# Two column blocks of the shared values by seven half-size products instead of eight, with the modulation sums 1024 columns wide

## The chip, the core and the metric

The kernel runs on one core of a Trainium2 chip. The metric is the time of one execution on the device in microseconds. Before the change the median of 3 runs is 1925.47 us (1925.35 to 1926.13).

## What is computed

A decoder trunk of two layers over 512 tokens and 2048 features, all float32. Layer A is a differential attention, layer B a forgetting attention that reads keys, values and gates projected once from the output of layer A. Cut to what matters here:

```python
def shared_kv(x, c_act, w_mod_kv, b_mod_kv, w_kv, b_f):
    mod = c_act @ w_mod_kv + b_mod_kv
    shift, scale = jnp.split(mod, 2, axis=-1)
    hk = x * (1.0 + scale[:, None]) + shift[:, None]
    kvf = hk @ w_kv
    k, v, zf = jnp.split(kvf, [B_WIDTH, 2 * B_WIDTH], axis=-1)
...
for l in range(DEPTH):
    mod = c_act @ w_mod[l] + b_mod[l]
    shift, scale, gate = jnp.split(mod, 3, axis=-1)
    h = x * (1.0 + scale[:, None]) + shift[:, None]
    y = diff_attention(h, ...) if l < N_A else forgetting_attention(h, ..., k_sh, v_sh, F_sh)
    x = layer_norm(DN_ALPHA * x + gate[:, None] * y, ln_g[l], ln_b[l])
```

`kvf` is a product of 512 x 2048 by 2048 x 4112: 2048 columns of keys, 2048 of values, 16 of gate logits. Each `mod` is a matrix-vector product over 2048 rows, which VectorE sums up beside the large products.

## The kernel before

Every large product is made of 128 x 128 x 512 matmuls in fp32r. For accuracy each operand is split into a rounded part and a rest (`hi`, `lo`), and `products` (L206) issues three matmuls: hi by hi, hi by lo, lo by hi. So a block of 512 columns costs 16 depth tiles x 4 token blocks x 3 = 192 matmuls.

`WeightStream` (L67) brings the weights, in the order of the list `ws.order`. One step is a tile `wst` of two depth tiles by 512 columns (512 KB, four buffers), loaded through the SP queue; ScalarE casts it to `whi` (L113), VectorE subtracts to get `wlo` (L114), three buffers each. `ws.get` keeps the splitting two steps ahead of the product.

`group` (L345) runs one column block: for each of 8 weight steps, 4 bursts of 6 matmuls. After each burst `tick` runs one waiting piece (attention, evacuations) and, where `bg` says so, some steps of `background`. That is `mod_stream` (L396): it loads 512 columns of a modulation weight and multiplies them into the accumulator `macc` on VectorE (L433), one depth tile per step. The first such stream, opened at L818, runs beside layer A's projections (the groups `qk[h]` and `vg[h]`) and makes the gate of layer A and the shift and scale of the keys and values. The second, opened in `open_n` (L1262), runs from layer A's output projection on and makes layer B's shift, scale and gate; part of its loads go through tiles `msk` of the pool `K`.

The normalised output of layer A is one tile `n`, 4 token blocks by 2048 columns. `build_half` (L1318) turns it on TensorE, scales it on ScalarE and splits it to `Hh`, `Hl`, and writes the turned values back to `n`; six of the 32 pieces go through DRAM in place of TensorE. `build_h` (L1373) reads the turned `n` once more for layer B.

The value columns are five blocks `vj`: 0, 512 and 1024 (512 wide), 1536 and 1800 (264 wide, the last with the gate logits). Below they are called V0 to V4, and the four key blocks `kj` K0 to K3. V0 is built by hand together with `build_half`; V1 to V4 (L1474) and K0 to K3 (L1477) are groups, in this order. The tile framework decides where each instruction stands on its engine, apart from those that are kept in program order; within an engine execution is in order, and a waiting instruction holds all behind it.

## Time and profile before

| what | us |
|---|---|
| median of 3 runs | 1925.47 |
| span of the profiled execution, first to last instruction | 1923.5 |
| difference, around the span | 1.97 |
| PE busy | 1910.4 |
| DVE (VectorE) busy | 1370.3 |
| ACT (ScalarE) busy | 732.9 |
| V1 to V4, from the end of V0 to the end of V4 | about 131 |

PE is TensorE's matmuls, PEld its weight loads, SP the queue that issues most DMAs. A view of windows gives busy time in a stretch, in us from the span's start; the number in brackets behind it counts instructions, and the last three numbers are the granted clock as a share of full speed, the share of time that the DMA engines were busy, and GB/s. A view of groups gives the busy sum, the mean duration in ns, and the idle time ahead of the group with what ended it. A timeline row gives start and duration. Matmuls overlap, so the duration of one is not the time it adds.

### The profile page before, as it was taken

To read this page: it belongs to the slowest core of one execution; us is meant where nothing else is said; L and a number is where in the kernel's file an instruction comes from. 1 tells how busy PE (TensorE), PEld (TensorE's weight loads), DVE (VectorE), ACT (ScalarE), POOL (GpSimd) and SP (SyncE) were. 2 spreads that over 40 slices of the span, in tenths; PEclk is the share of its full clock that TensorE was granted. 3 is DMA by queue.
4 is the path that set the end of the run, shared out by engine and by line. 5 is a ranking of instruction groups with operands and counts; after the bars stand their busy time and mean duration, and the time that the engine had idled before them with its cause. 6 is when DMAs were issued, how large, how long until landed. Compare 5 with 4: busy or idle time off the path is not lost.

```text
span 1923.5 us, 25879 instructions
## 1 busy us (share of the span) xinstructions
PE 1910.4 (99%) x8921; PEld 1593.5 (83%) x8921; DVE 1370.3 (71%) x2617; ACT 732.9 (38%) x1266; POOL 2.3 (0%) x11
## 2 busy tenths in 40 slices
PE   8999999999999999999999999999999999999998
PEld 7888888888888888888888898888888888888887
DVE  8993578777676868667675477777566666686768
ACT  3656344333232344521272232224344444453122
POOL 0000000000000000000000000000000000000000
PEclk9999999999999999999999999999999999999999
DMA  9993566676767675476557586775355555555622
GB/s 346 385 333 95 160 186 196 213 234 196 228 203 224 207 223 180 122 241 222 179 165 256 181 294 211 258 258 160 114 149 156 161 149 160 154 154 170 224 93 110
DMA packets 352275, 382.22 MB, mean 199 GB/s; under 512 B 77912, under 2 KB 256244, under 8 KB 351376
## 3 DMA queue, kind: packets, MB, share of 16 engines
q1 hardware_dynamic: 349040, 376.23, 62.2%
q10 hardware_dynamic: 3104, 4.35, 0.6%
q8 instruction: 70, 1.15, 0.3%
q14 instruction: 61, 0.50, 0.1%
HBM read 348.68 MB, written 31.80 MB: 198 GB/s over the span
## 4 chain that ended last, share of the span: by engine, by line
PE 97%; DVE 1%; SPq 1%; DMA 0%; issue 0%; ACT 0%; ACTq 0%
PE acc L208 27%; PE acc L210 27%; PE acc L209 27%; PE acc L720 4%; PE sc L720 2%; PE sc L210 1%; PE sc L209 1%; PE sc L208 1%; PE o L208 1%; PE o L210 1%; PE o L209 1%; PE o L720 1%; SPq L568 0%; PE tr L686 0%; PE tr L660 0%; DMA sms<-in_w_mod_dram 0%
## 5 line engine op out<-in xcount | busy, mean ns | idle before, releaser
L113 ACT CAST whi<-wst 128x1024 fp32r<-128x1024 f32 (+2 forms) x298 | 303.4, 1018 | 617.6 <-PE acc L210 310.1
L114 DVE TENSOR_TENSOR wlo<-wst,whi 128x1024 fp32r<-128x1024 f32 (+2 forms) x298 | 351.4, 1180 | 248.8 <-ACT whi L113 228.9
L208 PE MATMUL acc<-hh,whi 128*128 128x512 f32 x1184 | 462.9, 391 | 0.0
L209 PE MATMUL acc<-hl,whi 128*128 128x512 f32 x1184 | 461.6, 390 | 0.0
L210 PE MATMUL acc<-hh,wlo 128*128 128x512 f32 x1184 | 460.0, 390 | 0.0
L208 PE MATMUL acc<-whi,hh 128*128 128x512 f32 (+1 forms) x1104 | 418.5, 379 | 0.0
L209 PE MATMUL acc<-wlo,hh 128*128 128x512 f32 (+1 forms) x1104 | 416.7, 377 | 0.0
L210 PE MATMUL acc<-whi,hl 128*128 128x512 f32 (+1 forms) x1104 | 416.2, 377 | 0.0
L433 DVE SCALAR_TENSOR_TENSOR macc<-ms,cact,macc 128x512 f32<-128x512 f32 x307 | 229.0, 746 | 63.0 <-DMA ms<-in_w_mod_dram 44.5
L210 PEld LDWEIGHTS acc<-hh,wlo 128*128 128x128 f32 x1184 | 222.3, 188 | 47.4
L208 PEld LDWEIGHTS acc<-hh,whi 128*128 128x128 f32 x1184 | 222.3, 188 | 44.0 <-DVE sgb L1509 0.8
L209 PEld LDWEIGHTS acc<-hl,whi 128*128 128x128 f32 x1184 | 222.5, 188 | 42.3
L210 PEld LDWEIGHTS acc<-whi,hl 128*128 128x128 f32 x1104 | 207.3, 188 | 38.9
L208 PEld LDWEIGHTS acc<-whi,hh 128*128 128x128 f32 x1104 | 207.3, 188 | 37.2 <-DVE ztmp L1241 0.6
L209 PEld LDWEIGHTS acc<-wlo,hh 128*128 128x128 f32 x1104 | 207.4, 188 | 36.0
L618 DVE SCALAR_TENSOR_TENSOR sacc<-sms,cact,sacc 128x512 f32<-128x512 f32 (+1 forms) x128 | 89.9, 703 | 4.6 <-DMA sms<-in_w_mod_dram 0.7
L904 ACT ACTIVATE e<-e,mn 128x128 f32<-128x128 f32 (+3 forms) x64 | 36.0, 563 | 109.5 <-DVE mn L900 102.9
L1559 ACT ACTIVATE eb<-eb,mnb 128x128 f32<-128x128 f32 (+1 forms) x64 | 35.9, 561 | 72.7 <-DVE mnb L1556 72.4
L720 PE MATMUL acc<-wlo,hh 128*128 128x512 f32 x128 | 49.8, 398 | 0.0
L720 PE MATMUL acc<-whi,hl 128*128 128x512 f32 x128 | 49.3, 393 | 0.0
L720 PE MATMUL acc<-whi,hh 128*128 128x512 f32 x128 | 49.2, 393 | 0.0
L132 DVE TENSOR_TENSOR wlo<-wst,whi 128x768 fp32r<-128x768 f32 (+1 forms) x32 | 34.8, 1088 | 17.8 <-ACT whi L125 16.5
(336 smaller groups left out, 2096.6 us busy)
## 6 DMA issues: line engine op xcount, KB each, us to landing
wst<-in_a_w_in_dram SPq DMA_DIRECT2D x240, 256.0 KB
ms<-in_w_mod_dram SPq DMA_DIRECT2D x136, 256.0 KB
ms<-in_kv_w_mod_dram SPq DMA_DIRECT2D x64, 512.0 KB
wst<-in_b_w_in_dram SPq DMA_DIRECT2D x128, 256.0 KB
sms<-in_w_mod_dram SPq DMA_DIRECT2D x56, 512.0 KB
wst<-in_kv_w_dram SPq DMA_DIRECT2D x56, 512.0 KB
ms<-in_w_mod_dram SPq DMA_DIRECT2D x32, 512.0 KB
wst<-in_a_w_out_dram SPq DMA_DIRECT2D x32, 512.0 KB
```

The costliest lines, as they stand in the source:

```text
L113: self.nc.scalar.copy(hi[:, :, :w], st[:, :, :w])
L114: self.nc.vector.tensor_tensor(lo[:, :, :w], st[:, :, :w], hi[:, :, :w].bitcast(F32), op=ALU.subtract)
L132: self.nc.vector.tensor_tensor(lo[:, :, :w], st[:, :, :w], hi[:, :, :w].bitcast(F32), op=ALU.subtract)
L208: PE.matmul(dst, lhs[0], rhs[0], start=start, stop=False, skip_group_check=True)
L209: PE.matmul(dst, lhs[0], rhs[1], start=False, stop=False, skip_group_check=True)
L210: PE.matmul(dst, lhs[1], rhs[0], start=False, stop=stop, skip_group_check=True)
L433: ins = V.scalar_tensor_tensor(acc, w, cact[:, kt : kt + 1], acc, op0=ALU.mult, op1=ALU.add)
L618: V.scalar_tensor_tensor(acc, w, sc, acc, op0=ALU.mult, op1=ALU.add)
L720: PE.matmul(bank[n, bk], l, r, start=start, stop=stop, skip_group_check=True)
L904: S.activation(e[:, :w], e[:, :w], AF.Exp, bias=mn, scale=-1.0, accum_out=rs)
L1559: S.activation(e[:, :w], e[:, :w], AF.Exp, bias=mn, scale=-1.0, accum_out=rs)
```

## The change

V1 and V2 are now computed together as a product of 2 x 2 blocks, with seven half-size products instead of eight (Winograd's variant of Strassen's scheme). The activations are cut by tokens (blocks 0, 1 and 2, 3) and by even and odd depth tiles, the weights by even and odd depth tiles and by column block.

- `combine(s)` makes, for depth tiles 2s and 2s+1, four combinations of the activations (`sums`), split to `su` and `sl`. `su` takes the memory of `n`, which is therefore saved to `s_dram` and read back by `back_n`.
- `PairFirst` and `PairSecond` feed the weight stream: 4 steps of plain even tiles, 8 steps with one subtraction, 16 steps in pairs with three subtractions per pair, all on VectorE in the raw tile. During them every third raw tile is a `wsp` in the memory of the `ms` tiles, so that up to six are in use.
- `seven_products` has three phases: p1 (48 matmuls), p7 and p3 (96), and p2, p7, p1, p3 together (192).
- The order is now V0, V3, V4, the pair, K0 to K3. In the pair no `tick` runs, so no step of the modulation either.
- The modulation streams work on tiles of 1024 columns, with one `macc`, and layer B's gate has moved to the first stream. `bg` is set anew in all groups. The tiles `msk` are gone.
- `n` is four tiles of 512 columns, so `norm_a` issues two activations instead of one, two scalings instead of one, and four stores instead of one per token block.

```diff
+class PairFirst:
+    def load(self, nc, dst, kt):
+        n = kt // 2
+        if n < 4:
+            rows = self.src[4 * n * P : (4 * n + 4) * P, self.c0 : self.c0 + 512]
+            nc.sync.dma_start(dst, rows.rearrange("(k u p) n -> p k u n", p=P, u=2)[:, :, 0, :])
+        else:
+            rows = self.src[2 * (n - 4) * P : (2 * (n - 4) + 2) * P, self.c1 : self.c1 + 512]
+            nc.sync.dma_start(dst, rows.rearrange("(k p) n -> p k n", p=P))
+    def sums(self, nc, n, st, after):
+        if n >= 4:
+            nc.vector.tensor_tensor(st[:, 0, :], st[:, 1, :], st[:, 0, :], op=ALU.subtract)
...
+class PairSecond:
+    def load(self, nc, dst, kt):
+        n = kt // 2
+        c0 = self.cols[n % 2]
+        rows = self.src[2 * (n // 2) * P : (2 * (n // 2) + 2) * P, c0 : c0 + 512]
+        nc.sync.dma_start(dst, rows.rearrange("(k p) n -> p k n", p=P))
+    def sums(self, nc, n, st, after):
+        if n % 2 == 0:
+            other, minus = after(), partial(nc.vector.tensor_tensor, op=ALU.subtract)
+            minus(other[:, 0, :], other[:, 0, :], st[:, 0, :])
+            minus(other[:, 1, :], other[:, 1, :], other[:, 0, :])
+            minus(st[:, 0, :], st[:, 1, :], other[:, 1, :])
...
-            st = self.pool.tile([P, 2, 512], F32, name="wst", tag="wst", bufs=self.STAGES)
+            if self.paired(len(self.stage)) and len(self.stage) % 3 == 2:
+                st = self.spare()
+            else:
+                st = self.pool.tile([P, 2, 512], F32, name="wst", tag="wst", bufs=self.STAGES)
             job.load(self.nc, st, 2 * s)
             self.stage.append(st)
+    def paired(self, n):
+        return n < len(self.order) and isinstance(self.order[n][0], (PairFirst, PairSecond))
...
+        if isinstance(job, (PairFirst, PairSecond)):
+            self.load(self.done + 2)
+            job.sums(self.nc, s, st, lambda: self.stage[self.done + 1])
...
+            while self.paired(len(self.stage)) and self.paired(self.done) and len(self.stage) < self.done + self.STAGES + 1:
+                self.load(len(self.stage) + 1)
...
+    s_dram = dram.tile([4, P, TB, 512], F32, name="s_dram")
...
+    pair = PairFirst(kv_w, 2048 + 512, 2048 + 1024), PairSecond(kv_w, 2048 + 512, 2048 + 1024)
+    for j in [o[1] for o in oA] + [vj[0], vj[3], vj[4]]:
+        ws.add_job(j)
+    for j, steps in zip(pair, (12, 16)):
+        ws.add_job(j, steps)
+    for j in kj + bj + [o[1] for o in oB]:
         ws.add_job(j)
...
+        for k, (i, kt) in enumerate(todo):
+            load_upto(k if calm else k + ahead)
...
+                ins = V.tensor_scalar(acc, w, one, None, op0=ALU.mult)
+            else:
+                ins = V.scalar_tensor_tensor(acc, w, one, acc, op0=ALU.mult, op1=ALU.add)
+            tc.keep_in_program_order(ins)
+            if kt == 4:
+                while turned_sums:
+                    next(turned_sums.pop(0), None)
+            yield
+            if kt == KT - 1:
+                for half, steps in enumerate(segs[i][2]):
+                    turned_sums.append(steps(acc[:, 512 * half : 512 * half + 512]))
+                    next(turned_sums[-1])
+                    yield
...
+            ap, (
+                (gate_dram[0], w_mod[0], 2 * D, b_mod[0], (0.0,)), (gate_dram[1], w_mod[1], 2 * D, b_mod[1], (0.0,)),
+                (mod_dram[0], kv_w_mod, 0, kv_b_mod, (0.0, 1.0)),
+            ),
+        ),
+        lambda: ap.tile([P, 1024], F32, name="ms", tag="ms", bufs=2),
+        lambda: ap.tile([P, 1024], F32, name="macc", tag="macc", bufs=1),
+        1,
...
-    group(qk[2], False, lambda b, acc: keep(("qk", b), acc), bg=lambda k: k % 3 == 2)
+    group(qk[2], False, lambda b, acc: keep(("qk", b), acc), bg=lambda k: k % 4 == 3)
...
-    group(vg[2], True, keep_vg, bg=lambda k: k % 2)
+    group(vg[2], True, keep_vg, bg=lambda k: k % 3 == 1)
...
-        group(qk[h], False, evac, bg=lambda k: k % 2)
+        group(qk[h], False, evac, bg=lambda k: k % 3 == 1)
...
-        group(vg[h], True, evac_rest, bg=lambda k: 1 if k % 8 in (1, 3, 4, 5, 7) else 0, after_sub=early if h == A_HEADS - 1 else None)
+        group(vg[h], True, evac_rest, bg=lambda k: k % 2, after_sub=early if h == A_HEADS - 1 else None)
...
-            bg = (lambda n: 1 if n % 3 else 0) if layer == 0 and k in (1, 2) else 0
+            bg = (lambda n: n % 3 == 1) if layer == 0 and k in (1, 2) else 0
...
-            deep=range(50, 106),
-            new_deep=lambda: ktile("msk"),
+            vectors(pool, ((mod_dram[1], w_mod[1], 0, b_mod[1], (0.0, 1.0)),)),
+            lambda: pool.tile([P, 1024], F32, name="ms", tag="ms", bufs=3),
+            lambda: pool.tile([P, 1024], F32, name="macc", tag="macc", bufs=1),
+            2,
...
+    def combine(s):
+        cs = 256 * s, 256 * s + 256
+        whole = []
+        for q in range(2):
+            kt = 2 * s + q
+            f = npool.tile([P, T], F32, name="htmp", tag="htmp", bufs=2)
...
+                src = ncols(slice(0, TB), kt * P, (kt + 1) * P)
+                S.activation(f.rearrange("p (b t) -> p b t", t=P), src, AF.Identity, scale=sc, bias=sh)
+            whole.append((f[:, 0:256], f[:, 256:512]))
+        if s % 2:
+            nc.sync.dma_start(s_dram[s // 2], nt[s // 2])
+        sums = npool.tile([P, 4, 256], F32, name="sums", tag="tn", bufs=2)
+        (a11, a21), (a12, a22) = whole
+        s3, s4, s1, s2 = (sums[:, k, :] for k in range(4))
+        V.tensor_tensor(s1, a21, a22, op=ALU.add)
+        V.tensor_tensor(s2, s1, a11, op=ALU.subtract)
+        V.tensor_tensor(s3, a11, a21, op=ALU.subtract)
+        V.tensor_tensor(s4, a12, s2, op=ALU.subtract)
+        waiting.append((s, sums))
+        if s % 2:
+            t = npool.tile([P, 2, 4, 256], F32R, name="su", tag="n", bufs=4)
+            for k, (w, sums) in enumerate(waiting):
+                upper[w] = t[:, k]
+                S.copy(upper[w], sums)
+                lower[w] = [kpool.tile([P, 2, 256], F32R, name="sl", tag="K") for _ in range(2)]
+                for m, lo in enumerate(lower[w]):
+                    two = slice(2 * m, 2 * m + 2)
+                    V.tensor_tensor(lo, sums[:, two], upper[w][:, two].bitcast(F32), op=ALU.subtract)
+            waiting.clear()
...
+    def seven_products():
+        def add(dst, lhs, tiles, k, start=False, stop=False):
+            for b in both:
+                products(dst[b], lhs(b), (tiles[0][k], tiles[1][k]), start, stop)
...
+        p1 = [acc_bank() for _ in both]
+        for a in range(4):
+            tiles = ws.get(one, a)
+            if a < 2:
+                combine(6 + a)
+            for k in range(2):
+                s = 2 * a + k
+                add(p1, lambda b: plain(2 * s, b), tiles, k, s == 0, s == 7)
...
+        for b in both:
+            S.copy(first[b], p1[b])
+        p7 = [acc_bank() for _ in both]
+        p3 = [sc_bank() for _ in both]
+        for s in range(8):
+            tiles = ws.get(one, 4 + s)
+            add(p7, lambda b: combined(s, 0, b), tiles, 0, s == 0, s == 7)
+            add(p3, lambda b: combined(s, 1, b), tiles, 1, s == 0, s == 7)
+        diff = [npool.tile([P, T], F32, name="htmp", tag="htmp", bufs=2) for _ in both]
+        for b in both:
+            S.copy(diff[b], p3[b])
+            V.tensor_tensor(diff[b], p7[b], diff[b], op=ALU.subtract)
...
+        for s in range(8):
+            last = s == 7
+            ta = ws.get(two, 2 * s, 1)
+            add(p2, lambda b: plain(2 * s + 1, b), ta, 1, s == 0, last)
+            if s not in (0, 7):
+                add(p7, lambda b: plain(2 * s + 1, 2 + b), ta, 0)
+            tb = ws.get(two, 2 * s + 1, 1 if s in (0, 7) else 2)
+            add(p1, lambda b: combined(s, 3, b), tb, 1, stop=last)
+            if s in (0, 7):
+                add(p7, lambda b: plain(2 * s + 1, 2 + b), ta, 0, stop=last)
+            add(p3, lambda b: combined(s, 2, b), tb, 0, stop=last)
+            if last:
+                for b in both:
+                    V.tensor_tensor(first[b], p2[b], first[b], op=ALU.add)
...
+                us = [ktile("us") for _ in both]
+                for b in both:
+                    S.copy(us[b], p1[b])
+                for b in both:
+                    t = ktile("vt")
+                    V.tensor_tensor(t, p7[b], us[b], op=ALU.add)
+                    store(t, 2 + b, c0)
+                for b in both:
+                    t = ktile("vt")
+                    V.tensor_tensor(t, p3[b], us[b], op=ALU.add)
+                    store(t, b, c1)
+                    V.tensor_tensor(diff[b], diff[b], t, op=ALU.add)
+                    store(diff[b], 2 + b, c1)
...
+    def back_n():
+        new_n()
+        for f in range(4):
+            nc.sync.dma_start(nt[f], s_dram[f])
...
-    for g in range(1, 5):
-        group(vj[g], True, evac_v(g), bg=lambda k: k % 2)
+    group(vj[3], True, evac_v(3), bg=lambda k: k % 8 == 7, after_sub=lambda s: combine(s // 2) if s in (0, 2, 4) else None)
+    calm.append(1)
+    ws.spare = lambda: npool.tile([P, 2, 512], F32, name="wsp", tag="ms", bufs=3)
+    group(vj[4], True, evac_v(4), bg=lambda k: k in (3, 11), after_sub=lambda s: combine(3 + s // 2) if s in (0, 2, 4) else None)
+    seven_products()
+    calm.clear()
+    back_n()
...
         group(
-            kj[g], False, evac_k(g), bg=lambda k: 1 if k % 4 else 0,
+            kj[g], False, evac_k(g), bg=lambda k: k % 2 or k % 8 == 0,
```

How the instructions move. First TensorE, whose order rests on the products alone. Before, in V1, three matmuls per block and depth tile, all into the four banks `acc` (columns: line, operation, output, moving and stationary operand, size):

```order
L208 MATMUL acc<-whi,hh 128x512
L209 MATMUL acc<-wlo,hh 128x512
L210 MATMUL acc<-whi,hl 128x512
L208 MATMUL acc<-whi,hh 128x512
L209 MATMUL acc<-wlo,hh 128x512
```

And now, at the start of the pair's third phase (`p` are the banks of p2, `acc` of p1 and p7, `sc` of p3; `su`, `sl` are combined activations):

```order
L266 MATMUL p_10082<-whi,hh 128x512
L267 MATMUL p_10082<-wlo,hh 128x512
L268 MATMUL p_10082<-whi,hl 128x512
L266 MATMUL acc<-whi,su 128x512
L267 MATMUL acc<-wlo,su 128x512
L268 MATMUL acc<-whi,sl 128x512
L266 MATMUL acc<-whi,su 128x512
L267 MATMUL acc<-wlo,su 128x512
L268 MATMUL acc<-whi,sl 128x512
L266 MATMUL acc<-whi,hh 128x512
```

The form of the matmul is the same; a weight tile now serves 12 of them, where it served 24. In the whole program TensorE has 8817 matmuls and transposes, where it had 8865: 48 fewer, all of 512 columns.

Next VectorE. Before, between two weight splits of V2 it ran modulation steps (`macc`), and at the end of a sum its turning (`mturn`) and reduction (`mred`):

```order
L433 SCALAR_TENSOR_TENSOR macc<-msk,cact,macc 128x512 x2
L464 STREAM_TRANSPOSE mturn<-macc 128x512
L465 TENSOR_REDUCE mred<-mturn 128x16
L114 TENSOR_TENSOR wlo<-wst,whi 128x1024
L431 TENSOR_SCALAR macc<-msk,cact 128x512
L433 SCALAR_TENSOR_TENSOR macc<-msk,cact,macc 128x512
```

Now, in the third phase of the pair, the subtractions on raw tiles (L108 to L110) stand there:

```order
L169 TENSOR_TENSOR wlo<-wsp,whi 128x1024
L108 TENSOR_TENSOR wst<-wst,wsp 128x512
L109 TENSOR_TENSOR wst<-wst 128x512
L108 TENSOR_TENSOR wsp<-wsp,wst 128x512
L169 TENSOR_TENSOR wlo<-wst,whi 128x1024
L110 TENSOR_TENSOR wsp<-wsp,wst 128x512
L109 TENSOR_TENSOR wsp<-wsp 128x512
L169 TENSOR_TENSOR wlo<-wst,whi 128x1024
L110 TENSOR_TENSOR wst<-wst,wsp 128x512
L169 TENSOR_TENSOR wlo<-wsp,whi 128x1024
```

Per two splits there are three subtractions and no modulation step.

Last ScalarE, near the end of V0, where `build_half` feeds the product. Before, the build's activations and a weight cast:

```order
L1347 ACTIVATE htmp_9193<-sc,mod_b_7741,mod_a_7740 128x256
L1348 ACTIVATE hh<-sc,mod_b_7741,mod_a_7740 128x256
L1332 ACTIVATE hh<-n,mod_b_7741,mod_a_7740 128x256 x2
L113 CAST whi<-wst 128x1024
L1347 ACTIVATE htmp_9253<-sc,mod_b_7741,mod_a_7740 128x256
```

Now, at the same place (`sums` is the output of `combine`, L1483 its own activations):

```order
L1405 ACTIVATE htmp_9166<-sc,mod_b_7757,mod_a_7756 128x256
L1406 ACTIVATE hh<-sc,mod_b_7757,mod_a_7756 128x256
L1483 ACTIVATE htmp<-n,mod_b_7757,mod_a_7756 128x512 x2
L1499 CAST su<-sums 128x1024
L1390 ACTIVATE hh<-n,mod_b_7757,mod_a_7756 128x256
L168 CAST whi<-wst 128x1024
L1390 ACTIVATE hh<-n,mod_b_7757,mod_a_7756 128x256
L1405 ACTIVATE htmp_9226<-sc,mod_b_7757,mod_a_7756 128x256
```

The first activations of `combine` and the first cast to `su`, which waits until the store of the first quarter of `n` to `s_dram` has landed, stand ahead of the last pieces of the build.

172 lines of the change are left out of this document (88 added, 84 removed).

## The prediction

> **What bounds the kernel now.** The page comes first: its span, its busy times, and the chain that ended last.
>
> ```profile
> span 1923.5 us, 25879 instructions
> PE 1910.4 (99%) x8921; PEld 1593.5 (83%) x8921; DVE 1370.3 (71%) x2617; ACT 732.9 (38%) x1266; POOL 2.3 (0%) x11
> PE 97%; DVE 1%; SPq 1%; DMA 0%; issue 0%; ACT 0%; ACTq 0%
> ```
>
> TensorE is the bound from end to end: 97% of the chain. But a busy share of pipelined matmuls proves little, so the view of waits comes second, for TensorE: what did it wait for in the middle of the program?
>
> ```profile
> PE tr L241 <- DMA crow<-in_c_dram: 3.1, 1, 3.1
> PE sc L1339 <- ACT n L1314: 0.2, 1, 0.2
> ```
>
> These are the first and the seventh of its eight waits. Five lie before 195 us, in the preamble, two of 0.3 and 0.2 us behind 1330, where layer B runs. Between them, over the stages that the change touches, only the second of these rows is left: 0.2 us, once. So removing work from any other engine wins nothing, removing matmuls wins their pitch, and every new wait of TensorE is lost time.
>
> Third, the pitch. The timeline of TensorE in V1 gives start and duration; the two rows are 36 matmuls apart:
>
> ```profile
> 1059.82 0.39 PE L208 MATMUL acc<-whi,hh 128*128 128x512 f32 x1
> ...
> 1067.98 0.39 PE L208 MATMUL acc<-whi,hh 128*128 128x512 f32 x1
> ```
>
> (1067.98 − 1059.82) / 36 = 0.2267 us from start to start; the 0.39 us of a record overlaps its neighbours. As a cross-check, the last evacuations of V1 and of V2:
>
> ```profile
> 1063.42 0.59 ACT L1400 COPY vt<-acc 128x512 f32<-128x512 f32 x1 [0.77 <-PE acc L210]
> ...
> 1106.94 0.59 ACT L1400 COPY vt<-acc 128x512 f32<-128x512 f32 x1 [0.77 <-PE acc L210]
> ```
>
> They lie 43.52 us apart for 192 matmuls: 0.2267 again. A column block is pure pitch.
>
> Fourth, the windows: is there room beside TensorE? Columns: window, length, busy time of PE, PEld, DVE, ACT, POOL, clock, DMA share, GB/s.
>
> ```profile
> 455.00:502.00 47.00, 47.00 (x219) 39.27 (x218) 32.12 (x57) 13.46 (x22) 0.00 (x0) 1.00 0.74 230
> 980.00:1020.00 40.00, 39.78 (x191) 32.60 (x190) 24.73 (x50) 26.75 (x50) 0.00 (x0) 1.00 0.49 145
> 1064.00:1108.00 44.00, 44.00 (x201) 36.63 (x200) 21.22 (x26) 10.32 (x14) 0.00 (x0) 1.00 0.58 196
> 1108.00:1156.00 48.00, 48.00 (x390) 47.45 (x390) 38.05 (x53) 14.29 (x25) 0.00 (x0) 1.00 0.87 291
> 1288.00:1332.00 44.00, 44.00 (x195) 36.17 (x195) 38.52 (x69) 20.63 (x30) 0.00 (x0) 1.00 0.57 182
> ```
>
> They are one `vg` group of layer A, V0 with the build, V2, V3 with V4, and the last key block. The granted clock is 1.00 in each. Two rows matter as precedents: V3 and V4 use up a weight step in 2.9 us (16 in 46) and load 291 GB/s without a stall; the last key block has VectorE 88% busy without a stall.
>
> **The change part by part.** *Removed.* V1 and V2 took 384 matmuls, 384 × 0.2267 = 87.0 us. The seven products take 336 of the same form, 76.2 us. Gain **48 × 0.2267 = 10.88 us**. Nothing else on TensorE changes in number.
>
> The row that bears on a rule of the Trainium skill is the timeline above, 226.7 ns with a weight load before each matmul. "TensorE: Matmul & The Clock Gate", section "Back-to-back issue gap", puts a sustained stream of such pairs at about 131 ns for 512 columns; by that the estimate would be 48 × 0.131 = 6.3 us. The trace shows 226.7 over 36 and over 192 matmuls, so it decides; the sum is made with 10.88.
>
> *Added on VectorE and ScalarE in the pair.* The rows, from the groups by form (busy, mean ns):
>
> ```profile
> L114 DVE TENSOR_TENSOR wlo<-wst,whi 128x1024 fp32r<-128x1024 f32 x274 | 334.6, 1221 | 215.6 <-ACT whi L113 199.8 <-PE o L209 6.6 <-DMA e<-turned 4.0
> L113 ACT CAST whi<-wst 128x1024 fp32r<-128x1024 f32 x274 | 288.2, 1052 | 576.0 <-PE acc L210 277.3 <-PE acc L209 211.8 <-issue 50.5
> L114 DVE TENSOR_TENSOR wlo<-wst,whi 128x528 fp32r<-128x528 f32 x16 | 11.3, 707 | 16.1 <-ACT whi L113 11.9 <-DMA msk<-in_w_mod_dram 4.1
> L1241 DVE TENSOR_TENSOR ztmp<-acc,gate 128x512 f32<-128x512 f32 x24 | 15.7, 681 | 1.0 <-PE acc L210 0.9
> L1349 DVE TENSOR_TENSOR hl<-htmp,hh 128x256 fp32r<-128x256 f32 x24 | 10.0, 417 | 7.2 <-ACT hh L1348 7.2
> ```
>
> The pair has 28 weight steps where V1 and V2 had 16. VectorE does 31 splits there, with the first three of K0: 31 × 1.221 = 37.9 us. To these come 8 + 24 subtractions on raw tiles and about 12 operations of 512 columns from `combine` and the evacuations: 44 × 0.681 = 30.0 us. Together 67.9 of 76.2 us, 89%; the last key block ran at 88%. In exchange no modulation step stands in the pair. ScalarE casts 31 × 1.052 = 32.6 us plus some 8 of copies: not a bound. The cover for all of this is TensorE: 12 matmuls per step, 2.72 us. Without it each step costs what VectorE needs above 2.72 us; that is the first rival.
>
> *Added beside V3 and V4.* Six calls of `combine`: 24 additions of 256 columns at 0.417 and 12 subtractions at about 0.68 make 18.2 us of VectorE, with 16 splits of 528 columns (11.3) and 6 modulation steps (7.7, price below) 37 us, with the build's last operations some 42 of 46 us. The row of before has 38.05 there with no stall. So nothing, as long as the splits stay two steps ahead.
>
> *Switches of the banks.* Four places are new: first to second phase, second to third, third to K0, and V4 to the pair; a fifth is V0's end, where ScalarE's queue now holds a cast to `su` that waits for a store, and behind it the last build pieces, on which TensorE waits. Nearest row: the V0 window, PE 39.78 of 40.00, so 0.22 us lost at a similar hand-over. Bounds per place: zero (V2's window, 44.00 of 44.00) and 0.77 + 0.59 us, the wait and the copy of an evacuation row. I take 0.22 × 5 = **1.1 us**; range 0 to 6.8.
>
> *Modulation.* A 1024-wide step has its price from the nearest row of that shape:
>
> ```profile
> L433 DVE SCALAR_TENSOR_TENSOR macc<-ms,cact,macc 128x512 f32<-128x512 f32 x307 | 229.0, 746 | 63.0 <-DMA ms<-in_w_mod_dram 44.5 <-DMA ms<-in_kv_w_mod_dram 15.4
> L1751 DVE SCALAR_TENSOR_TENSOR z<-z,lrstd,ln_b 128x1024 f32<-128x1024 f32 x6 | 7.4, 1281 | 0.1
> ```
>
> 1.281 us for what took 2 × 0.746: VectorE saves 0.21 us on each of 192, 40 us in all, off the bound, so worth nothing. The first stream gets longer: a `vg` group has 16 wide steps in place of 20 narrow ones, so VectorE goes from 32.1 to about 32.1 − 18 × 0.746 + 16 × 1.281 = 39.2 of 47 us (18 is that window's count). Below VectorE's 88%, so nothing from work alone. Its loads grow from 10 to 16 per group, 0.524 MB each: 230 GB/s × 47 us = 10.8 MB become 14.0 MB, 297 GB/s. The row's own ratio, 230 at a share of 0.74, would be full at 311. That is close, and it is the third rival. In K0 and K1, 20 of 32 bursts carry a step: 4.2 + 20 × 0.524 = 14.7 MB in 43.5 us, 338 GB/s, where V3 and V4's ratio (291 at 0.87) is full at 334. I take zero, the nearest row being the 291 that left nothing waiting, and the rows of the new tiles being twice as long; if 334 is the limit, 14.7 / 0.334 = 44.0 us, +0.5 us each, and at 311 it is 47.3, +3.8 each.
>
> *The memory of `n`.* Four stores and four reads of 1.05 MB. The reads stand among the third phase's weight loads: 8.4 + 4.2 MB in 43.5 us, 290 GB/s, as V3 and V4 had without a stall. A read waits in SP's queue until the matmuls on `su` are done, and holds the weight loads behind it; six raw tiles are the cover. Zero taken, up to 3 us if a load comes one 2.72 us step late. `norm_a`'s additional instructions stand beside the last products of layer A's output projection; bounded by the 0.2 us of the waits above.
>
> **Sum.** 1925.47 − 10.88 + 1.1 = **1915.7 us**. The profiled execution has 1923.5 of span and 1.97 around it, which is the median; its span would become 1913.7.
>
> **The rivals.**
>
> *1. A serial chain in the pair (about no change).* Per two steps of the third phase: three subtractions, then cast and split of both tiles. If subtraction, cast and split are not overlapped, that is 3 × 0.681 + 2 × (1.052 + 1.221) = 6.59 us against 5.44 of matmuls: 1.15 × 8 = 9.2 us; the second phase 0.681 + 2.273 = 2.95 against 2.72: 8 × 0.23 = 1.9 us. Time 1915.7 + 11.1 = 1926.8. For it: the groups show that VectorE's splits mostly wait for the cast (199.8 us). Against it: there are three `whi` and `wlo` buffers, six raw tiles, and two steps of lead, so the cast of one tile can lie beside the split of another.
>
> *2. Partial stalls:* the upper bounds of the switches (6.8), K0 and K1 short of DMA, a late read of `n`. Two or three of these in part give 1917.5 to 1921.6; K0 and K1 at 311 GB/s, +7.6, give 1923.
>
> *3. Slower: the two `ms` tiles of the first stream.* A load can start only when the step before last is done. Rows of before, from the timeline, from issue to the step that waits for it, and from the view of waits between 195 and 800 us:
>
> ```profile
> 486.88 0.37 SPq L409 DMA_DIRECT2D ms<-in_kv_w_mod_dram  x1
> ...
> 491.23 0.75 DVE L433 SCALAR_TENSOR_TENSOR macc<-ms,cact,macc 128x512 f32<-128x512 f32 x1 [1.80 <-DMA ms<-in_kv_w_mod_dram]
> ...
> DVE macc L433 <- DMA ms<-in_kv_w_mod_dram: 15.4, 13, 2.8
> DVE macc L433 <- DMA ms<-in_w_mod_dram: 6.7, 5, 3.0
> ```
>
> 4.35 us for 512 KB. Two steps then take 4.35 + 1.28 + about 0.4 of issue; eight such pairs are 48.2 us against the group's 47. VectorE waits in order, so splits, evacuations and attention stand behind a late step, and TensorE follows. At 4.35 us that is 1.2 us in each of 6 groups, +7, about no change (1923); from about 4.6 us it is slower: at 5.0, 53.4 − 47 = 6.4 × 6 = 38 us, 1954. For it: the crowding to 297 GB/s. Against it: in the 605 us of that stage VectorE waited for such loads for 22 us in 18 waits, so most land sooner than they are wanted.
>
> *4. The other prices of a matmul.* By the mean record of 0.39 us the gain would be 18.7 us, 1907.9; the pitch excludes it, bar a gain by other means. That the change does not do what it says is excluded by the count: 48 fewer matmuls.
>
> **How the numbers follow.** 0.2% (3.85 us) is about what a measurement of this kernel can tell from no change, so faster means below 1921.6 and slower above 1929.3.
>
> - Forecast, 1914.0 to 1917.5: 0.53.
> - Rival 2, 1917.5 to 1921.6: 0.20.
> - About no change, 1921.6 to 1929.3, rival 1 (0.10) and the milder half of 3 with K0 and K1 (0.05): 0.15.
> - Rival 3 in full, above 1929.3: 0.10.
> - Below 1914: 0.02.
>
> Faster 0.75, same 0.15, slower 0.10. The range goes from 1914.0 to 1924.5 and leaves out about 0.19: 0.02 below, 0.10 above 1929.3, and half of no change.
>
> **What would show it.** If the steps hold: the pair, from V4's last matmul to K0's first, lasts 76 to 77 us; the pitch in it is 0.227; TensorE's waits name at most the bank switches, each under a microsecond; VectorE is some 89% busy in the pair. Rival 1 shows as TensorE waiting for `wlo`, evenly spaced at about 1 us per two steps. Rival 3 shows as VectorE's `macc` waiting for `ms` for hundreds of microseconds, and layer A's groups longer than 47 us. DMA crowding shows as K0 and K1 longer than 43.5 us at a DMA share near 1. The forecast is wrong if layer A's stage ends later than before, since nothing there can win time.

## The result

The changed kernel takes 1936.01 us, median of 4 runs (1934.26 to 1937.67), where the kernel before took 1925.8 beside it. The ratio is 1.0054, interval 1.004 to 1.0069. It is slower by 10.2 us, where 9.8 us of gain had been forecast. The profiled execution has a span of 1932.4 us; it is the shortest of the four, 1934.26 us.

The page of the changed kernel, the same lines as before:

```profile
span 1932.4 us, 25569 instructions
PE 1909.8 (99%) x8873; PEld 1584.0 (82%) x8873; DVE 1393.9 (72%) x2531; ACT 762.8 (39%) x1312; POOL 2.3 (0%) x11
PE 86%; DVE 5%; DMA 5%; SPq 2%; issue 1%; ACT 1%; ACTq 0%; DVEq 0%
```

TensorE has 48 instructions fewer, as announced (8873 for 8921 on the pages), and still looks 99% busy. The chain tells more: TensorE's share fell from 97% to 86%, and VectorE and DMA now stand in it with 5% each. The view of TensorE's waits, of which these rows are new or longer:

```profile
PE o L266 <- ACT ah L1010: 4.8, 5, 2.3
PE acc L267 <- DVE wlo L169: 1.0, 2, 0.8
PE acc L266 <- ACT hh L1390: 1.0, 2, 0.5
PE acc L266 <- DVE sg L922: 0.7, 3, 0.4
```

The largest is not in the pair. `ah` (L1010) and `sg` (L922) belong to layer A's attention and evacuations, which the change did not rewrite. Windows of layer A's attention stage, 345 us to the output projection, in the kernel before:

```profile
345.00:790.00 445.00, 445.00 (x2052) 371.07 (x2052) 332.40 (x677) 165.15 (x301) 0.00 (x0) 1.00 0.69 209
```

And after, with the pair in the second row:

```profile
345.00:803.00 458.00, 451.99 (x2059) 372.00 (x2058) 353.92 (x640) 163.28 (x304) 0.00 (x0) 1.00 0.76 236
...
1082.00:1162.00 80.00, 79.03 (x340) 62.84 (x339) 57.45 (x68) 33.42 (x38) 0.00 (x0) 1.00 0.71 229
```

The stage takes 458 us instead of 445, and TensorE is idle for 6.0 of them. The rest of the loss doesn't show as idle time: 1.6 us of it are matmuls at half the clock behind one stall (last section), and the remainder is in short gaps, since the record of a matmul, 0.39 us, outlasts its pitch. So the measure used below is the **loss over the pitch**: the sum, over a stage, of the time from one matmul's start to the next, less the pitch of its shape in an undisturbed stretch (0.2267 us for 512 columns, 0.120 for 264, 0.1133 for 256; other widths are left out). It is worked out from the timeline of TensorE, with a noise of some tenths:

```
loss over the pitch, us       before  after
layer A, 345 to 803 us           3.8   15.5
V0's end to K0, 1000 to 1206     0.6    8.7
last key blocks, 1206 to 1340    0.6    0.4
```

11.7 us more are lost in layer A and 8.1 in the value stage; less the 10.9 of the 48 products that is +8.9, as much as the spans differ. (The bounds are in each kernel's own time.)

What a stall in layer A looks like, by the timeline of the changed kernel around 433 us (SP's issue, VectorE, ScalarE, TensorE):

```profile
427.46 0.34 SPq L469 DMA_DIRECT2D ms<-in_w_mod_dram  x1
...
432.76 1.28 DVE L479 SCALAR_TENSOR_TENSOR macc<-ms,cact,macc 128x1024 f32<-128x1024 f32 x1 [1.54 <-DMA ms<-in_w_mod_dram]
433.96 0.55 DVE L956 CUSTOM_DVE_ANT_0 e<-sc,bias 128x384 f32<-128x384 f32 x1
...
434.61 0.62 ACT L960 ACTIVATE e<-e,mn 128x384 f32<-128x384 f32 x1 [2.26 <-DVE mn L956]
435.22 0.28 ACT L1010 CAST ah<-e 128x128 fp32r<-128x128 f32 x1
435.56 0.39 PE L266 MATMUL o<-vh,ah 128*128 128x256 f32 x1 [2.29 <-ACT ah L1010]
```

Read from the top: a load issued at 427.46 is used 5.3 us later. VectorE waits 1.54 us for it, and the softmax step behind it starts only when the 1.28 us sum is over. ScalarE waits for that step, with the cast `ah` behind it, and TensorE waits for `ah`. All four wait in order; none is short of time on average.

### The profile page after: what moved, and what is told of

It reads as the page before. It is cut to its first block, busy times and chain, and to the rows that moved or that the text cites. A ratio compares the mean times of both kernels' runs of the same rounds, so it can differ in the third digit from the quotient of the medians.

```text
span 1932.4 us, 25569 instructions
## 1 busy us (share of the span) xinstructions
PE 1909.8 (99%) x8873; PEld 1584.0 (82%) x8873; DVE 1393.9 (72%) x2531; ACT 762.8 (39%) x1312; POOL 2.3 (0%) x11
## 4 chain that ended last, share of the span: by engine, by line
PE 86%; DVE 5%; DMA 5%; SPq 2%; issue 1%; ACT 1%; ACTq 0%; DVEq 0%
PE acc L266 23%; PE acc L267 23%; PE acc L268 23%; PE acc L771 4%; PE sc L771 2%; PE sc L268 1%; PE sc L267 1%; PE sc L266 1%; DMA ms<-in_w_mod_dram 1%; PE o L266 1%; PE o L268 1%; DVE wlo L169 1%; PE o L267 1%; PE o L771 1%; DMA turned<-e 1%
## 5 line engine op out<-in xcount | busy, mean ns | idle before, releaser
L266 PE MATMUL acc<-whi,hh 128*128 128x512 f32 (+1 forms) x1008 | 382.1, 379 | 1.1 <-ACT hh L1390 1.0
L267 PE MATMUL acc<-wlo,hh 128*128 128x512 f32 (+1 forms) x1008 | 379.6, 377 | 0.2 <-DVE wlo L169 0.2
L268 PE MATMUL acc<-whi,hl 128*128 128x512 f32 (+1 forms) x1008 | 379.1, 377 | 0.4 <-DVE hl L1391 0.4
L479 DVE SCALAR_TENSOR_TENSOR macc<-ms,cact,macc 128x1024 f32<-128x1024 f32 x180 | 230.2, 1279 | 59.7 <-DMA ms<-in_w_mod_dram 39.1
L266 PEld LDWEIGHTS acc<-whi,hh 128*128 128x128 f32 x1008 | 189.4, 188 | 36.2 <-ACT hh L1390 1.7
L268 PEld LDWEIGHTS acc<-whi,hl 128*128 128x128 f32 x1008 | 189.3, 188 | 35.8 <-DVE hl L1391 1.2
L267 PEld LDWEIGHTS acc<-wlo,hh 128*128 128x128 f32 x1008 | 189.5, 188 | 32.4 <-DVE wlo L169 0.6
```

The costliest lines, as they stand in the source:

```text
L266: PE.matmul(dst, lhs[0], rhs[0], start=start, stop=False, skip_group_check=True)
L267: PE.matmul(dst, lhs[0], rhs[1], start=False, stop=False, skip_group_check=True)
L268: PE.matmul(dst, lhs[1], rhs[0], start=False, stop=stop, skip_group_check=True)
L479: ins = V.scalar_tensor_tensor(acc, w, one, acc, op0=ALU.mult, op1=ALU.add)
```

## The experiments

Each table of loss gives layer A (345 to 803 us) and the value stage (1000 to 1206 us) of the profiled execution. Layer A's program is the same in the changed kernel ("after"), `v_plain`, `late_store`, `p_nocomb` and `p_nosub`, and lost 15.5, 16.0, 13.5, 12.7 and 22.2 us there. So one profile's loss in layer A spreads over 9.5 us, and smaller differences say little without the medians. The profiled execution can also lie at the end of the range: it is the longest one for `ms3` (1931.11 us) and `p_nosub` (1938.03), the shortest for `p_nocomb` (1926.2).

**Without the loads, without the sums.**

```diff
# a_noload, first stream
...
+                if ahead == 1 and len(loaded) >= 2:
+                    loaded.append(two[len(loaded) % 2])
+                    continue
# a_nosum, first stream
+                n = 64 if ahead == 1 else 1024
-                ins = V.scalar_tensor_tensor(acc, w, one, acc, op0=ALU.mult, op1=ALU.add)
+                ins = V.scalar_tensor_tensor(acc[:, 0:n], w[:, 0:n], one, acc[:, 0:n], op0=ALU.mult, op1=ALU.add)
```

> Leaves out: in the first modulation stream only the first two ms tiles are loaded, and all 128 steps work on them, so layer A's gate, layer B's gate and the key-value shift and scale are wrong; VectorE's work stays the same. Between 345 and 803 us TensorE lost 15.4 us over its pitch in the changed kernel, 3.5 before. Theory LOADS (VectorE waits in its queue for ms tiles, 41 us there against 20 before, and the attention behind it is late): the loss goes back to about 3.5, so 1936.0 - 12 = 1924 us. Theory WORK (21 us more of VectorE work in pieces of 1.28 us stands ahead of the attention's softmax, whatever the loads do): the loss stays, 1933 to 1936 us. Theory PAIR (the loss is in the seven products): 1936 us.

> Leaves out: in the first modulation stream the multiply-adds work on 64 of 1024 columns, so its sums are wrong; all loads stay. Theory LOADS: VectorE still waits for ms tiles, though the tiles come free 1.2 us sooner; most of the loss stays, 1930 to 1935 us. Theory WORK: VectorE is relieved of some 140 us, the loss in layer A goes to about 3.5 us, 1924 us. Theory PAIR: 1936 us.

Measured: 1922.03 us (ratio 0.998, 0.997 to 0.9989) and 1924.22 us (0.9994, 0.9985 to 1.0004). The window of layer A without loads:

```profile
345.00:803.00 458.00, 458.00 (x2113) 381.70 (x2113) 362.61 (x656) 168.57 (x310) 0.00 (x0) 1.00 0.39 117
```

And without sums:

```profile
345.00:803.00 458.00, 456.89 (x2111) 380.98 (x2110) 268.70 (x656) 169.07 (x313) 0.00 (x0) 1.00 0.76 237
```

TensorE is full in both; layer A loses about 4 and 5 us. WORK falls: with VectorE as busy as ever (362.6 us) the loss is gone. But LOADS in its simple form falls too: with all the traffic (237 GB/s) and short sums it is gone as well, though VectorE then waits for its loads even longer, 76.4 us in 46 waits. Either half alone is harmless; it takes the waits and the long sums together. Two tiles would do that: the next load can't start before the sum on the tile before has ended. These two runs suggest it; the third tile below tests it.

**Layer B's gate back in the second stream; the pair undone.**

```diff
# g2_back
-                (gate_dram[0], w_mod[0], 2 * D, b_mod[0], (0.0,)), (gate_dram[1], w_mod[1], 2 * D, b_mod[1], (0.0,)),
+                (gate_dram[0], w_mod[0], 2 * D, b_mod[0], (0.0,)),
-            vectors(pool, ((mod_dram[1], w_mod[1], 0, b_mod[1], (0.0, 1.0)),)),
+            vectors(pool, ((mod_dram[1], w_mod[1], 0, b_mod[1], (0.0, 1.0)), (gate_dram[1], w_mod[1], 2 * D, b_mod[1], (0.0,)))),
-        group(vg[h], True, evac_rest, bg=lambda k: k % 2, ...)
+        group(vg[h], True, evac_rest, bg=lambda k: k % 3 == 1, ...)
# v_plain (and V1, V2 back in the order of the weights)
-    group(vj[3], ...); group(vj[4], ...); seven_products(); back_n()
+    for g in (1, 2):
+        group(vj[g], True, evac_v(g))
+    group(vj[3], True, evac_v(3), bg=lambda k: k % 8 == 7)
+    group(vj[4], True, evac_v(4), bg=lambda k: k in (3, 11))
```

> Layer B's gate goes back to the second stream, behind shift and scale; in layer A the groups run 11 of 32 bursts with a step instead of 16 (vg). The pair stays. Theories LOADS and WORK agree: the loss in layer A goes from 15.4 to 4 to 6 us, 1925 to 1927 us, unless the key blocks, which now carry 32 steps more, lose some of it. Theory PAIR: 1936 us, no change.

> The pair is undone: V1 and V2 are plain groups of 192 products without a modulation step, in the old order of the value blocks; the modulation stays as changed. 48 products more are 10.9 us. The trace shows 6.3 us lost from V0's end to K0 in the changed kernel, so LOADS and WORK expect the pair to be worth 10.9 - 6.3 + at most 1: 1936.0 + 4.5 = 1940 to 1942 us. Theory PAIR (the pair costs more than it saves): 1926 us or less.

Measured: g2_back 1936.0 us (1.0052), layer A's loss 6.4, so that stage is healed, but the key blocks lose 7.1 us instead of 0.4 and the stage behind them 5.2 instead of 2.0. v_plain 1938.96 us (1.0066), value stage 2.0: the pair is worth some 3 us, not 10.9, and PAIR falls. All of the change but the pair costs 13.5 us, of which the traces put 12 into layer A.

**A third tile; another queue.**

```diff
# ms3 (and the turned sum in the pool K, to make room)
-        lambda: ap.tile([P, 1024], F32, name="ms", tag="ms", bufs=2),
+        lambda: ap.tile([P, 1024], F32, name="ms", tag="ms", bufs=3),
-        1,
+        2,
# ms_pool
-                nc.sync.dma_start(loaded[-1], ...)
+                (nc.gpsimd if ahead == 1 else nc.sync).dma_start(loaded[-1], ...)
```

> All loads and all sums of the first modulation stream stay; its ms tiles are three instead of two, and loads are issued two steps ahead (room for the third tile: the turned sum moves to the pool K, the tile of ones loses unused columns). Without its loads (a_noload) and without its sums (a_nosum) layer A's loss fell alike, from 15.4 to 3.7 and 4.8 us. Theory CYCLE (two tiles: load, sum, next load, one after the other; either half removed breaks it): a third tile brings the loss to 4 to 6 us, 1925 to 1927 us in all. Theory TRAFFIC (64 loads more crowd the DMA queues and VectorE, whatever the number of tiles): the loss stays at 12 to 16 us, 1934 to 1937 us.

> Two tiles as in the changed kernel; the loads of the first modulation stream are issued on the POOL queue instead of SP. Theory CYCLE: VectorE still waits for each load, the loss in layer A stays above 10 us, 1933 to 1937 us. Theory SP (a load that waits for its tile holds SP, and behind it the weight loads and attention's reads of the turned scores, for which ScalarE's cast waited 0.6 to 1.75 us at three of the stalls): the loss falls to 4 to 7 us, 1925 to 1928 us.

Measured: ms3 1927.58 us (1.0007, 0.9998 to 1.0017), ms_pool 1968.35 us (1.0226). VectorE's waits for these loads between 345 and 803 us in the changed kernel:

```profile
DVE macc L479 <- DMA ms<-in_w_mod_dram: 22.0, 21, 2.2
DVE macc L479 <- DMA ms<-in_kv_w_mod_dram: 19.4, 20, 2.9
```

And in ms3:

```profile
DVE macc L479 <- DMA ms<-in_kv_w_mod_dram: 5.5, 4, 2.5
DVE macc L479 <- DMA ms<-in_w_mod_dram: 5.4, 5, 2.0
```

41.4 us became 10.9 with the same traffic (234 GB/s) and the same work (VectorE 356.2 us busy), and 8.4 us of the time came back: CYCLE holds for most of it. (ms3 also moves the turned sum to another pool; no run has that alone.) In the changed kernel the 41 loads that VectorE waited for were used 5.0 us (median) after their issue.

SP falls by the same pair of runs. These are the waits of SP's queue, in the changed kernel and then in ms3:

```profile
SPq L469 <- DVE macc L479: 74.1, 49, 5.6
SPq L469 <- DVE macc L479: 85.2, 52, 6.0
```

Loads that wait for their tile hold SP no less in ms3, and yet the loss shrinks. ms_pool, which frees SP from them, is far worse, but it doesn't isolate SP: each load now starts 0.3 us behind its sum instead of 0.03, and the granted clock averages 0.97 between 345 and 803 us, where the changed kernel has 1.00. Its timeline shows the cycle bare, each issue right behind a sum:

```profile
499.55 0.53 POOL L469 DMA_DIRECT2D ms<-in_w_mod_dram  x1 [1.80 <-DVE macc L479]
501.73 1.28 DVE L479 SCALAR_TENSOR_TENSOR macc<-ms,cact,macc 128x1024 f32<-128x1024 f32 x1 [1.85 <-DMA ms<-in_w_mod_dram]
503.31 0.53 POOL L469 DMA_DIRECT2D ms<-in_w_mod_dram  x1 [3.23 <-DVE macc L479]
505.41 1.28 DVE L479 SCALAR_TENSOR_TENSOR macc<-ms,cact,macc 128x1024 f32<-128x1024 f32 x1 [1.26 <-DMA ms<-in_w_mod_dram]
506.99 0.53 POOL L469 DMA_DIRECT2D ms<-in_w_mod_dram  x1 [3.15 <-DVE macc L479]
```

One sum per 3.7 us; the 16 steps that the change asks of a `vg` group of 47 us would take 59 at that pace.

ms3 still loses 11.6 us in layer A by its profile, in another way. VectorE of ms3 at one of two stalls, where TensorE waited 2.08 us for `sg`:

```profile
498.36 1.28 DVE L479 SCALAR_TENSOR_TENSOR macc<-ms,cact,macc 128x1024 f32<-128x1024 f32 x1 [1.32 <-DMA ms<-in_w_mod_dram]
499.68 1.31 DVE L515 STREAM_TRANSPOSE mturn<-macc 128x512 f32<-128x512 f32 x2
500.90 0.65 DVE L516 TENSOR_REDUCE mred<-mturn 128x16 f32<-128x512 f32 x1
501.47 1.22 DVE L169 TENSOR_TENSOR wlo<-wst,whi 128x1024 fp32r<-128x1024 f32 x1
502.60 0.42 DVE L262 TENSOR_TENSOR vl<-acc,vh 128x256 fp32r<-128x256 f32 x1
```

A 1024-wide sum ends with two turnings (`mturn`) and two reductions (`mred`), and here that fell on the evacuations of `vg` (`vl`, `sg`).

**The place of the steps.**

```diff
# shift, ms3_shift
-    group(qk[2], ..., bg=lambda k: k % 4 == 3)
+    group(qk[2], ..., bg=lambda k: k % 3 == 1)
# quiet, ms3_quiet: as above, and
-    group(vg[2], ..., bg=lambda k: k % 3 == 1)
+    group(vg[2], ..., bg=lambda k: k % 3 == 1 and k < 26)
-        group(qk[h], ..., bg=lambda k: k % 3 == 1)
+        group(qk[h], ..., bg=lambda k: k % 5 in (1, 3))
-        group(vg[h], ..., bg=lambda k: k % 2, ...)
+        group(vg[h], ..., bg=lambda k: k % 2 and k < 26, ...)
```

> Two ms tiles as in the changed kernel; only the first group of the stream runs 11 steps instead of 8, so that every later end of a 1024-wide sum (two turnings, two reductions, 2.8 us on VectorE) comes three steps sooner. Theory CYCLE: no real change, the loss in layer A stays 11 to 16 us, 1933 to 1937 us. Theory BURST alone (ends of sums that fall on the evacuations of a vg group): 1926 to 1929 us.

> Three tiles and the same shift. In ms3 the waits for loads fell from 41 to 11 us, but two stalls of 2.1 us stayed, at 502 and 694 us, each with some 1.6 us of slower matmuls behind it, where a sum ends beside the evacuations of vg. Theory CYCLE and BURST together: both stalls go, layer A loses 4 to 5 us, 1919 to 1922 us. CYCLE alone: other stalls in their place, 1926 to 1929 us.

> The same steps with two ms tiles, as in the changed kernel. Theory CYCLE (two tiles are the cause): VectorE waits for loads as before, some 40 us, and the attention's casts are late: 1932 to 1936 us. Theory QUEUE alone (only the place of the steps matters): 1922 to 1926 us.

> Three ms tiles, and in the vg groups no modulation step in the last 6 of 32 bursts, where the evacuations stand (steps: 11 in qk[2], 9 in vg[2], 13 in every later qk and vg). In ms3_shift one stall of 2.3 us was left at 408 us, in front of it a multiply-add that waited 1.6 us for its load with the evacuations vl and sg behind it. Theory QUEUE (whatever holds a modulation step holds the evacuations behind it in VectorE's queue): layer A loses 4 to 5 us instead of 10, 1921 to 1924 us. If the stalls only move to the attention's casts: 1926 to 1929 us.

```
            us       loss A  value stage
shift       1939.47    18.5       7.6
quiet       1935.6     15.8       9.1
ms3         1927.58    11.6       9.0
ms3_shift   1928.11    10.2       6.7
ms3_quiet   1927.35     8.6       7.0
```

(For shift the measure leaves out a stall of 1.7 us behind a matmul of 384 columns.) With two tiles no place helps: shift is 3.5 us above the changed kernel, above what any theory expected, and quiet is level with it. With three the two stalls of ms3 go away under the shift, as BURST says, but one of 2.3 us comes at 408 us, and ms3_quiet still has two of 1.2 and 1.7. The times of the last three don't differ. So two tiles are the main cause, QUEUE alone falls with quiet, and the expected 1919 to 1924 us were missed. BURST is borne out for the two stalls it named: ms3_store, without the shift, has both again, and neither ms3_shift nor ms3_shift_store nor ms3_shift_plain has them. (Only the later of the two, at 694 us, has the slower matmuls behind it that the expectation gives to both.)

**The stores; combine; the subtractions.**

```diff
# late_store, ms3_store, ms3_shift_store
-            nc.sync.dma_start(s_dram[s // 2], nt[s // 2])
+            tc.keep_in_program_order(nc.sync.dma_start(s_dram[s // 2], nt[s // 2]))
# p_nocomb: combine() returns at once, combined() gives plain(2 * s + k % 2, b), no back_n()
# p_nosub: sums() of PairFirst and PairSecond do nothing
```

> The four stores to s_dram are kept behind the reads of the turned n in SP's queue. In the changed kernel TensorE lost 2.7 us between 1000 and 1030 us and 1.3 between 1030 and 1060, waiting for hh, which waited for n from turned_n, issued 0.5 us behind a 1 MB store. Theory STORE: these 4 us fall to about 1, 1933 us in all; casts to su come later, and the pair's second phase must not wait for them. Otherwise: no change, 1936 us.

> ms3 and late_store together. CYCLE and STORE: both gains, 1922 to 1924 us, with 2 to 3 us still lost in the pair. TRAFFIC: 1932 to 1934 us.

> The same with the stores to s_dram behind the reads of the turned n. In the changed kernel and beside it the store order moved the loss from the build (3 us less) to the pair's second phase (1 to 3 us more): 0 to 2 us less than ms3_shift, 1918 to 1922 us.

> Leaves out: the combinations of the activations; the products that should use su and sl use plain hh and hl, n is not saved nor read back, so the values of columns 512 to 1535 are wrong. The changed kernel lost 4.0 us from 1000 to 1060 us (V0's end and V3's start; before 1.7 over the same place) and 4.7 from 1060 to 1206. Theory COMBINE (its stores, casts and sums stand ahead of the build's last pieces): the first loss falls to 1.5 to 2. Theory ORDER (V3 with half the time per weight step follows V0 now): it stays at 4. The second loss is the subtractions' or the loads' and stays at 3 to 5 by either.

> Leaves out: the 32 subtractions on raw weight tiles, so the values of columns 512 to 1535 are wrong; all loads, casts and splits stay. Theory CHAIN (rival 1 of the prediction: subtraction, cast, split one after the other): the loss from 1060 to 1206 us, 4.7 in the changed kernel, falls to 1 or less, and VectorE has 22 us less to do there. Theory RAW (the raw tiles are loaded late): 3 to 5 stay. The loss at V0's end stays at 4.

```
                  us      1000-1060  1060-1206
after             1936.01       4.0        4.7
late_store        1935.69       3.5        7.8
p_nocomb          1932.07       2.2        1.7
p_nosub           1932.26       4.2        2.8
```

Putting the stores back takes 0.4 to 1.0 us off the build in the three runs and adds up to 3.9 behind it, and nothing is won (ms3_store 1929.76, ms3_shift_store 1929.16): STORE falls. Without combine's work both losses shrink and the pair, 79.8 us in the changed kernel, takes 76.8, so COMBINE holds for about half of V0's end, and it reaches into the pair. Part of the latter is the matmuls themselves, which run slower on combined operands (last section). Of the 2.2 us that stay at V0's end, where the kernel before lost 0.3, ORDER may have its part: v_plain, which has neither combine nor V3 behind V0, loses 1.3 there. No run separates that. Without the subtractions TensorE is never idle in the pair, by the window of p_nosub:

```profile
1090.00:1167.00 77.00, 77.00 (x334) 62.45 (x333) 41.09 (x40) 31.67 (x33) 0.00 (x0) 1.00 0.73 241
```

Of its 2.8 us, 1.3 are the slower matmuls, and 0.65 stand at K0, where the gate logits' rows come 0.5 us late. Its pair takes 77.8 us, 2.0 less than the changed kernel's; the median is 3.7 us lower, on a spread of 10 us. So the subtractions cost some 2 to 4 us, not the 11.1 of rival 1. Even that isn't a steady price: shift, ms3_shift and ms3_quiet keep all the subtractions, and their pair takes 77.9 to 78.0 us. RAW isn't excluded either, since VectorE's longest wait in the changed kernel's pair, 3.5 us, was for a raw tile. What makes the stall come in one schedule and not in the other is open.

**The pair beside a milder modulation; the gate behind it once more.** `ms3_shift_plain` is ms3_shift with the edit of v_plain; `g2_back3` is g2_back with three tiles, `n % 2` for `n % 3 == 1` in layer A's output projection, and the fold of layer B's shift and scale six bursts later.

> ms3_shift with the pair undone (V1, V2 as plain groups, old order, no step of the modulation in them): 48 products more, 10.9 us, and without the 6 to 7 us that the traces show lost from V0's last products to K0. The pair's worth by the pitch alone: 10.9 us more than ms3_shift; by the traces: 3 to 5 us more, 1923 to 1926 us.

> Layer B's gate in the second stream as in g2_back, but with three ms tiles in the first stream, 16 steps instead of 11 in the two groups of layer A's output projection, and the fold of layer B's shift and scale six bursts later in K2, since g2_back lost 7 us in the key blocks where TensorE waited for that fold. Theory QUEUE: layer A loses 4 to 5 us (11 steps per group, three tiles), the key blocks 1 to 4: 1920 to 1925 us, the first version not slower than before. If the second stream is too long for the key blocks whatever the place of the fold: 1926 to 1930 us, with the loss there instead of in layer A.

Measured: 1931.26 us, 3.2 above ms3_shift, value stage 1.1: the pair is worth 3 us again. g2_back3: 1932.05 us. Its layer A loses 4.3 us, about as much as the kernel before; the key blocks lose 9.0. TensorE's waits there:

```profile
PE tr L1355 <- DMA mrow<-mod_dram: 3.9, 1, 3.9
PE tr L525 <- DVE mred L516: 2.6, 1, 2.6
```

TensorE stands at the end of the sum (L525, 2.6 us) and at the fold (L1355, 3.9 us), which turns the finished shift and scale of layer B into columns. The sums themselves aren't late: they end at 1238 us, sooner than the 1272 of the changed kernel. What comes late is the read for the fold, which SP issues behind the loads of the gate:

```profile
1281.28 5.39 SPq L469 DMA_DIRECT2D ms<-in_w_mod_dram  x3
1286.71 0.43 SPq L63 DMA_DIRECT2D wst<-in_kv_w_dram  x1
1288.92 0.33 SPq L469 DMA_DIRECT2D ms<-in_w_mod_dram  x1
1289.30 0.42 SPq L1353 DMA_DIRECT2D mrow<-mod_dram  x1
```

TensorE went on at 1293.72, 4.4 us after that issue; in the changed kernel, where no gate is loaded there, the read was issued 7.6 us ahead of the fold. Between 1230 and 1300 us SP waited 31.2 us for tiles that the sums still held. Before, the stream had V1 and V2 to run beside, with a step in every second of their 64 bursts, and the pair took those away; that they would have been place enough for the gate isn't shown. No version that leaves nothing out is faster than the kernel before; the best, ms3_quiet, ms3 and ms3_shift, can't be told from it.

## Why the prediction was wrong

The windows of a `vg` group and of the `qk` group behind it, first of the kernel before, then of the changed kernel:

```profile
455.00:501.00 46.00, 46.00 (x214) 38.45 (x213) 31.12 (x54) 12.91 (x20) 0.00 (x0) 1.00 0.75 235
501.20:549.70 48.50, 48.50 (x225) 40.48 (x225) 39.11 (x91) 18.75 (x39) 0.00 (x0) 1.00 0.66 196
460.50:507.00 46.50, 46.41 (x214) 38.31 (x212) 33.48 (x46) 12.03 (x18) 0.00 (x0) 1.00 0.80 242
507.00:558.00 51.00, 49.85 (x226) 40.68 (x227) 41.77 (x89) 19.30 (x41) 0.00 (x0) 1.00 0.76 242
```

- **The count** held: 48 products less. **The pitch** of 0.2267 us held for plain operands, and the losses add up to the measured span only with the full 10.9: 11.7 + 8.1 - 10.9 = 8.9 us. It did not hold for the 192 products of the pair that take a combined operand. Theirs is 0.233 (last section), some 1.3 us that no term of the sum had.
- **The modulation's first stream, costed at zero, is the step that failed.** The text worked out 39.2 of 47 us of VectorE and 297 GB/s of DMA for a `vg` group and found room in both. There was even more room, since a `vg` group ran 12 or 13 sums, not 16: some of the steps are the ends of sums. VectorE was busy 33.5 to 34.1 of 46 us in the three middle `vg` groups, at 242 to 263 GB/s. Neither average decided. The cost is 11.7 us, and most of it, 8.7, came in four `qk` groups, 49.3 to 52.8 us long where they had been 48.4 to 49.1, while the `vg` groups got longer by less than 1 us each. What decided was rival 3, given a chance of 0.10 in full and 0.05 in a milder form with K0 and K1: loads took 5.0 us to their use, beyond the 4.6 from which it was to decide. Its price, 38 us, was too high, because it let every `vg` group run 16 sums at the period of the two tiles. A `vg` and a `qk` group together ran 25 sums; at (5.0 + 1.28) / 2 = 3.1 us each, an estimate, these are 78 of their 97 us. So the stream keeps up, and the loss comes from single late steps with softmax or evacuations behind them. The forecast argued against the rival with 22 us of waits in the trace of before; those 22 us were with 10 loads per `vg` group, where the changed kernel ran 12 or 13.
- **The switches, 1.1 us in the sum, were mis-sized.** The value stage lost 8.1 us more than before, above the range's 6.8. V0's end, one of five places at 0.22, cost 3.7, about half of it through combine's work, which the scheduler put among the last pieces of the build. The pair, from 1081.97 to 1161.76 us, took 79.8 us, not 76 to 77: 1.3 by the slower matmuls, the rest by short stalls. The casts, stores and sums were counted as covered by V3 and V4, and a part of them was not there.
- **VectorE in the pair** was forecast 89% busy and was 72% (57.5 of 80 us). 27 splits and 40 operations of 512 columns fell into it, where 31 and 44 were counted, and records of neighbours overlap, by 3 us in all. It was late there all the same, by 0.8 us once.
- **K0 and K1** were feared for DMA and cost next to nothing: 0.9 us in K0, most of it the logits' rows, and 0.4 behind it, as forecast.
- **Rival 1** was the wrong size: 2 to 4 us by p_nosub, and not evenly spaced.

## What to carry to other kernels

A background stream with two tiles can't run two steps in less than one load and one sum: compare that period, with the loads' time under the new traffic, to the time that two slots give, before comparing busy shares. In an in-order engine the cost of a late step is the cost of what stands behind it. When a faster product removes time in which other work was hidden, that work needs a new place, and its price belongs into the sum; here the pair won 3 us, and the rest of the change, the moved modulation above all, cost 6 to 13.5.

## What the runs showed of the hardware

**A stall of 2.3 us cost 1.6 us more behind it.** The rows of the changed kernel behind the wait of 2.29 us, from the timeline of TensorE:

```profile
436.87 0.63 PE L267 MATMUL acc<-hl,whi 128*128 128x512 f32 x1
437.29 0.63 PE L268 MATMUL acc<-hh,wlo 128*128 128x512 f32 x1
437.72 0.63 PE L266 MATMUL acc<-hh,whi 128*128 128x512 f32 x1
```

And the windows ahead of the stall, behind it, and later:

```profile
425.00:432.50 7.50, 7.50 (x35) 6.25 (x35) 5.57 (x13) 3.15 (x6) 0.00 (x0) 1.00 0.84 268
436.30:439.30 3.00, 3.00 (x9) 2.41 (x8) 0.00 (x0) 0.00 (x0) 0.00 (x0) 0.50 0.86 261
440.00:444.00 4.00, 4.00 (x20) 3.37 (x19) 2.48 (x7) 1.95 (x4) 0.00 (x0) 1.00 0.85 287
```

The granted clock was 0.50 for about 3 us and the pitch 0.427 us, so some 1.6 us more were lost while TensorE counted as busy. The Trainium skill, "TensorE: Matmul & The Clock Gate", section "Part 1: The HAM clock gate", says that the clock falls to half after an idle window of about 3.4 us and comes back after a busy one of the same length. The halved clock and the length agree; the idle time here was shorter, 2.3 us. Its length alone doesn't decide: of two waits of 2.08 us in ms3 the one at 694 us was followed by slow matmuls and the one at 502 was not. In g2_back a wait of 2.3 us was and one of 2.7 was not, and in g2_back3 a wait of 3.9 us was and one of 2.6 was not. What else decides is not shown here.

**A matmul on a combined operand took 0.233 us.** The rows are from the pair's second phase, 30 matmuls apart, first of the changed kernel, then of p_nocomb, where the same products take plain operands:

```profile
1097.00 0.39 PE L266 MATMUL acc<-whi,su 128*128 128x512 f32 x1
1104.00 0.39 PE L266 MATMUL sc<-whi,su 128*128 128x512 f32 x1
...
1089.29 0.39 PE L266 MATMUL sc<-whi,hh 128*128 128x512 f32 x1
1096.09 0.39 PE L266 MATMUL acc<-whi,hh 128*128 128x512 f32 x1
```

7.00 / 30 = 0.233 us against 6.80 / 30 = 0.227, without any wait. p_nosub, ms3_shift and ms3_quiet have the longer pitch on these operands too. What about the operands `su` and `sl` costs the 6 to 7 ns is open.
